# Recording the second half of a transformer block, with its buffers, for the builder that orders all engines

## The chip, the cores and the metric

The kernel runs on one core of one Trainium2 chip. A core has a matrix engine (TensorE, PE in the profile; its weight loads are PEld), a vector engine (VectorE, DVE), a scalar engine (ScalarE, ACT), a general engine (GpSimd, POOL) and SyncE (SP), which here only issues DMA transfers. Each engine works its own queue strictly in the order written by the program; engines wait for each other by semaphores. The metric is the device time of one execution in microseconds (us), lower is better; several executions are timed and their median is given.

## What is computed

One layer (DEPTH is 1) on x of 512 tokens by 1024. Cut to what matters here:

```python
h = h + jnp.concatenate([o_a, o_b, o_c], axis=-1) @ w_out[i]
h = h + conv_gated_mlp(rms_norm(h, ln_ffn[i]), w_up[i], conv_w[i], conv_b[i], w_down[i])
gate = jax.nn.sigmoid(rms_norm(h, ln_ple[i]) @ w_ple_gate[i])
h = h + (p[i] @ w_ple_proj[i]) * gate
```

Ahead of the first line stand a norm, one input projection and three kinds of attention (8 pairs of heads, A0 to C2). The MLP projects up to 2 x 2816 columns, puts a causal depthwise convolution of width 3 over the tokens, takes silu(gate) * val and projects down.

## The kernel before

**Precision by pairs.** Each matrix operand is split into a rounded high part and a low rest: `split` (line 408) has ACT write `hi` and DVE write `lo` = raw - `hi`. A product is then three matmuls, hi·hi, hi·lo, lo·hi (`mm3`, line 425). Weights land in raw tiles (`wraw`) from the SP queue, and PE reads `whi` and `wlo`. `Th` and `Tl` are the pairs of the activations, transposed.

**First half, up to line 1045.** While a `Plan` object is open, every call of an engine is recorded as an `Op` with the regions that it reads and writes. `Plan.due` gives PE's operations due times in program order (with a table of shifts per group, `SHIFT`), and works back from them for the others. `Plan.solve` then walks a model with prices per operation: of the operations that are ready at an engine it takes the one that is due first, and it lets DVE and POOL not use SBUF at once (`port`). `PLAN.pop().emit()` (line 1045) issues everything in that order. This Plan ends with the sixth of eight input blocks (k = 0 to 5) of the output projection.

**The end of the output projection, norm, projection of p (lines 1040 to 1184).** `last_out(t)` adds the input blocks k = 6 and 7 for token tile t (4 tiles of 128), both column halves n, in PSUM banks z and s. `ffn_norm(t)` computes the MLP's norm; `ffn_cols(t)` transposes it into `Th` and `Tl`; `ple_unit(n, t)` multiplies p with `w_ple_proj` and stores the result in DRAM (`pp_d`). Only PE is kept in program order here (`pe.pinned`); a scheduler of the framework places the work of ACT, DVE, POOL and SP, also in front of recorded work of the first half.

**MLP and gate (lines 1186 to 1886).** 22 column blocks f. Most are plain; f = 5, 10 and 15 are computed with seven instead of eight block products (`seven_weights`), whose sums of weights are made by adding DMAs and POOL. The down projection (`Down`, `down_weights`) uses the same scheme and names its blocks a1, t1, t2, b2, t3, a2, t4; its last part (phases 2 and 3) has weights in tiles `dn...`, sums of them by POOL, and adds each product onto `h` (`add_h`, on DVE, from a PSUM bank). `xh`/`xl` and `g..ah`/`g..al` are the pairs of the MLP's inner values. `cols3` transposes the finished `h`, and `gate` multiplies with `w_ple_gate`, takes the sigmoid and adds. Here a planner (`trial`, line 1856, and the loop behind it) orders tasks by hand-set costs, and the order in which it calls them is the order of all five queues (line 1869).

**Buffers.** Six raw tiles go round: four `wraw`, and two that reuse the room of one `whi` and one `wlo` (`in_turn`, line 394); seven of eight hi and lo tiles go round for splits. The pool `mp` (line 1049) opens in the room of the first half's pool; its tag `conv` has ten buffers, handed out in turn as new tiles.

Of the kernel before, what the change touches and what calls it, by code (L numbers as in the profile page):

```python
# [15 lines left out]
P = 128  # L16
D = 1024
S = 512
# [49 lines left out]
}  # L68


class Op:


# [5 lines left out]
class Plan:  # L79
# [2 lines left out]
    WRITES = ("out", "accum_out")  # L82
    LEAD = {"act": 0.035, "dve": 0.035, "pool": 0.095, "pe": 0.055, "sp": 0.1}

    def __init__(self, clock, there):
        self.group = "first"
        self.clock, self.there, self.ops, self.mem = clock, [(v.tensor.name, self.region(v), t) for v, t in there], [], {}

    @staticmethod
    def region(v):  # L90
        size = 2 if v.dtype == BF16 else 4
        (row, pn), *rest = [tuple(x) for x in v.ap]
        if v.tensor.space == bass.MemoryType.DRAM:
            return 0, 1, 0, 1
# [10 lines left out]
    def add(self, eng, name, a, k):  # L105
        op = Op(eng, name, a, k)
        named = [("out" if i == 0 and "out" not in k else "in", v) for i, v in enumerate(a)] + list(k.items())
        seen = [(key in self.WRITES, v) for key, v in named if hasattr(v, "tensor")]
        op.outs, op.ins = [v for w, v in seen if w], [v for w, v in seen if not w]
        op.ready = 0.0  # L110
        for w, v in sorted(seen, key=lambda x: x[0]):
            r = self.region(v)
            p0, p1, c0, c1 = r
            log = self.mem.setdefault(v.tensor.name, [])
            for other, (q0, q1, d0, d1), t in self.there:
                if other == v.tensor.name and c0 < d1 and d0 < c1:
                    op.ready = max(op.ready, t)
            keep = []
            for rec in log:
                other, w2, (q0, q1, d0, d1) = rec  # L120
                hit = p0 < q1 and q0 < p1 and c0 < d1 and d0 < c1
                if hit and (w or w2) and other is not op:
                    op.deps.append(other)
                if not (w and other is not op and p0 <= q0 and q1 <= p1 and c0 <= d0 and d1 <= c1):
                    keep.append(rec)
            keep.append((op, w, r))
            self.mem[v.tensor.name] = keep
        op.deps = list(dict.fromkeys(op.deps))
        op.pos, op.group = len(self.ops), self.group
        self.ops.append(op)  # L130
        self.price(op)

    def price(self, op):
        e, k = op.eng.name, op.k
        n = self.width(op.outs[0])
        cols = sum(1 for v in op.ins if self.width(v) == 1) - (op.name == "reciprocal")
        acc = "accum_out" in k
        op.move = 0
        if e == "pe":
            if op.name == "transpose":  # L140
                op.busy = 0.109
            else:
                op.busy = n * 0.0004556 + 0.001 if op.ins[0].dtype == F32R else n * 0.0017
            op.lag = 0.165
        elif e == "act":
            op.busy, op.lag = 0.06 + n * 0.00088 + (0.18 + 0.04 * cols if acc else 0.09 * cols), 0.1
        elif e == "dve":
            n = max([n] + [self.width(v) for v in op.ins])
            op.busy, op.lag = 0.07 + n * 0.001045 * (1 + (op.name == "tensor_tensor_scan")) + 0.06 * cols, 0.083
        elif op.name == "dma_start":  # L150
            op.move = n * 4 * op.outs[0].shape[0]
# [15 lines left out]
    ENGINES = ("dve", "pe", "act", "pool", "sp")  # L167

    def due(self, shift):
        t = 4.5  # L170
        for op in self.ops:
            if op.eng.name == "pe":
                op.dl = t + shift.get(op.group, 0.0)
                t += op.busy
        for op in reversed(self.ops):
            if op.eng.name != "pe":
                spent = op.busy + op.lag + 0.05 + (op.move / self.HW + 2.0 if op.move else 0.0)
                op.dl = min([q.dl for q in op.next], default=t) - spent

    def solve(self):  # L180
# [11 lines left out]
        while True:  # L192
# [44 lines left out]
        assert len(order) == len(self.ops)  # L237
        return order

    def emit(self):  # L240
        for op in self.ops:
            for d in op.deps:
                d.next.append(op)
        for op in self.choose():
            op.eng.now(op.name, op.a, op.k)

    def choose(self):
        self.due(SHIFT)
# [4 lines left out]
def kernel(ctx: ExitStack, tc: tile.TileContext, x, xt0, xt, pt_in, small, g_ffn_in, bias_c,  # L253
# [13 lines left out]
    ps = ctx.enter_context(tc.tile_pool(name="ps", bufs=1, space=bass.MemoryType.PSUM))  # L267

    PLAN = []

    class Engine:

# [20 lines left out]
    class Fixed:  # L293
# [5 lines left out]
        def tile(self, shape, dt, tag, bufs=1, name=None):  # L299
# [11 lines left out]
            kind, t = self.made[key]  # L311
            v = t[: shape[0], :n]
            if kind != dt:
                v = v.bitcast(dt)
            if len(shape) == 3:
                v = v.rearrange("p (a b) -> p a b", a=shape[1])
            return v

        def again(self, tag, bufs, dt):
# [74 lines left out]
    def in_turn(what, n):  # L394
        ring = RING[what]
        if len(ring) < n:
            tag = what
# [6 lines left out]
        return ring[-1]  # L404

    def raw_tile():
        return in_turn("raw", NRAW)
# [650 lines left out]
    nc.sync.dma_start(out=g_ffn, in_=g_ffn_in)  # L1058
    HN = {}

    def ffn_norm(t):

        token_stats(t, h[:, t, :], mtmp(BF16, 2, f"n2_sq{t}"))
        HN[t] = []
        for g in range(2):
            c = slice(g * S, (g + 1) * S)
            hn = mtmp(F32, 1, f"n2_hn{t}_{g}")
            dve.scalar_tensor_tensor(hn, h[:, t, c], rstd[:, t, 2:3], g_ffn[:, c], ALU.mult, ALU.mult)
            HN[t].append(hn)

    def ffn_cols(t):
        for g in range(2):
# [5 lines left out]
    def ple_cols():  # L1078

        pin = [mtmp(F32, 1, f"pin{k}") for k in range(2)]  # L1080
        for k in range(2):
            nc.sync.dma_start(out=pin[k], in_=pt_in[k])
# [7 lines left out]

    def ple_load(n, k):
        t = raw_tile()
        nc.sync.dma_start(out=t[:, :S], in_=w_ple_proj[k * P : (k + 1) * P, n * S : (n + 1) * S])
        WPP[n, k] = split(t, S)

    def ple_unit(n, t):
# [6 lines left out]
        nc.sync.dma_start(out=pp_d[t, n], in_=pp)  # L1103

    U = {}

# [6 lines left out]
    Xh, Xl = (mp.tile([P, 4, 4, H], F32R, tag=tag, name=tag) for tag in ("xh", "xl"))  # L1113
    for f in SEVEN:
        w = bass.AP(cols.tensor, cols[:, C_CONV0 + NF + f : C_CONV0 + NF + f + 1].offset, [cols.ap[0], [2 * NF, 3]])
        nc.gpsimd.tensor_scalar(w, w, -1.0, 1.0, ALU.mult, ALU.mult)
    XA = {}

    def keep_cols(t, g, pt):
# [467 lines left out]
    old("pin")  # L1587
    old("left")
    xa = old("left")
    old("conv")  # L1590
    HNS = {(2, 0): old("conv"), (2, 1): old("conv")}
    old("conv", 3)
    HNS.update({(3, 0): old("conv"), (3, 1): old("conv")})
    old("conv", 2)
    for tag in ("z", "s", "t", "o"):
        old(tag, COUNT[tag])
    old("raw", 4)
# [352 lines left out]
```

## Time and profile before

| | us |
|---|---|
| median of 3 runs (lowest, highest) | 721.74 (720.13, 722.8) |
| the profiled execution | 721.91 |
| its span, first to last instruction | 720.0 |
| PE busy in the span | 702.6 |
| DVE busy | 557.5 |
| ACT busy | 389.8 |
| POOL busy | 268.3 |
| mean granted TensorE clock | 0.997 |

All engines run at once, so busy times don't add up. In a row of the timeline stand the start, the duration, the engine, the line and the operation with output and inputs; in brackets the idle time of the engine just before, and what ended it. Line 286 is the one line through which all recorded and wrapped calls go, so the names of tiles tell operations apart. Matmuls overlap: a 512-column one lasts about 0.39 us, while the next one starts 0.23 us after it.

### The profile page before, as it was taken

To read this page: it belongs to the slowest core of one execution; us is meant where nothing else is said; L and a number is where in the kernel's file an instruction comes from. 1 tells how busy PE (TensorE), PEld (TensorE's weight loads), DVE (VectorE), ACT (ScalarE), POOL (GpSimd) and SP (SyncE) were. 2 spreads that over 40 slices of the span, in tenths; PEclk is the share of its full clock that TensorE was granted. 3 is DMA by queue.
4 is the path that set the end of the run, shared out by engine and by line. 5 is a ranking of instruction groups with operands and counts; after the bars stand their busy time and mean duration, and the time that the engine had idled before them with its cause. 6 is when DMAs were issued, how large, how long until landed. Compare 5 with 4: busy or idle time off the path is not lost. (4 is left out here: it accounts for less than half of the span.)

```text
span 720.0 us, 11793 instructions
## 1 busy us (share of the span) xinstructions
PE 702.6 (98%) x4204; PEld 633.6 (88%) x4204; DVE 557.5 (77%) x1090; ACT 389.8 (54%) x745; POOL 268.3 (37%) x355
## 2 busy tenths in 40 slices
PE   7999999999999999899999999999999999989997
PEld 7999999999999887698888899888998888889886
DVE  7788898888887755758789778797988789986552
ACT  6657685575676644745555444454445443434821
POOL 3687676847666621203003331113410023280400
PEclk9999999999999999999999999999999999999999
DMA  9533552314112245454536325541362323113441
GB/s 323 201 99 89 142 136 91 103 53 130 68 55 66 67 124 160 140 175 111 162 104 145 103 89 178 130 117 45 103 203 77 117 66 118 42 55 102 154 124 59
DMA packets 36951, 83.22 MB, mean 116 GB/s; under 512 B 4215, under 2 KB 6263, under 8 KB 36893
## 3 DMA queue, kind: packets, MB, share of 16 engines
q1 hardware_dynamic: 32844, 73.52, 32.1%
q0 software_dynamic: 3760, 8.66, 6.5%
q8 instruction: 33, 0.54, 0.3%
q10 hardware_dynamic: 288, 0.30, 0.1%
q14 instruction: 26, 0.21, 0.1%
HBM read 74.19 MB, written 4.21 MB: 109 GB/s over the span
## 5 line engine op out<-in xcount | busy, mean ns | idle before, releaser
L286 PE MATMUL z<-whi,Th 128*128 128x384 f32 (+2 forms) x356 | 123.6, 356 | 6.0 <-ACT whi L286 4.5
L286 ACT CAST whi<-wraw 128x768 fp32r<-128x768 f32 (+2 forms) x132 | 98.5, 766 | 52.4 <-POOL wraw L286 23.2
L286 PE MATMUL z<-wlo,Th 128*128 128x384 f32 (+2 forms) x356 | 122.0, 352 | 0.0
L286 PE MATMUL z<-whi,Tl 128*128 128x384 f32 (+2 forms) x356 | 121.7, 351 | 0.0
L286 DVE TENSOR_TENSOR wlo<-wraw,whi 128x768 fp32r<-128x768 f32 (+2 forms) x114 | 105.0, 936 | 16.6 <-ACT whi L286 16.2
L286 PEld LDWEIGHTS z<-whi,Th 128*128 128x128 f32 x356 | 67.5, 190 | 10.7 <-ACT whi L286 4.5
L286 PEld LDWEIGHTS z<-whi,Tl 128*128 128x128 f32 x356 | 67.1, 189 | 4.6 <-DVE Tl L286 0.4
L286 PEld LDWEIGHTS z<-wlo,Th 128*128 128x128 f32 x356 | 67.3, 190 | 3.3
L286 PE MATMUL z<-Th,whi 128*128 128x512 f32 (+1 forms) x180 | 66.3, 368 | 1.4 <-ACT pps L286 1.4
L286 PE MATMUL s<-Th,whi 128*128 128x512 f32 (+1 forms) x180 | 66.2, 368 | 0.0
L286 PE MATMUL z<-Tl,whi 128*128 128x512 f32 (+1 forms) x180 | 66.1, 367 | 0.0
L286 PE MATMUL s<-Tl,whi 128*128 128x512 f32 (+1 forms) x180 | 66.0, 367 | 0.0
L286 PE MATMUL z<-Th,wlo 128*128 128x512 f32 (+1 forms) x180 | 66.0, 367 | 0.0
L286 POOL TENSOR_TENSOR wraw<-wraw,wraw 128x768 f32<-128x768 f32 (+1 forms) x14 | 26.1, 1877 | 107.0 <-DVE wlo L286 93.6
L286 PE MATMUL s<-Th,wlo 128*128 128x512 f32 (+1 forms) x180 | 66.0, 366 | 0.0
L286 ACT ACTIVATE e<-e,st 128x128 f32<-128x128 f32 (+3 forms) x80 | 44.6, 559 | 15.9 <-DVE st L286 15.5
L286 POOL TENSOR_TENSOR rs<-rs,nhalf 128x4 f32<-128x4 f32 x40 | 43.2, 1090 | 4.9 <-DVE rs L286 1.4
L286 PE MATMUL t<-wlo,g_ah 128*128 128x256 f32 x150 | 42.4, 282 | 0.3 <-DVE wlo L286 0.3
L286 PE MATMUL t<-whi,g_ah 128*128 128x256 f32 x150 | 42.3, 282 | 0.3 <-DVE h L286 0.3
L286 DVE SCALAR_TENSOR_TENSOR c<-z,cols,c 128x511 f32<-128x511 f32 (+1 forms) x38 | 28.4, 748 | 18.0 <-ACT c L286 17.4
L286 PE MATMUL t<-whi,g_al 128*128 128x256 f32 x150 | 42.3, 282 | 0.0
L286 PEld LDWEIGHTS z<-Th,whi 128*128 128x128 f32 x180 | 33.8, 188 | 7.9 <-ACT pps L286 1.8
(337 smaller groups left out, 1955.9 us busy)
## 6 DMA issues: line engine op xcount, KB each, us to landing
wraw<-in_w_up_dram SPq DMA_DIRECT2D x33, 384.0 KB, 3.8
wraw<-in_w_in_dram SPq DMA_DIRECT2D x28, 384.0 KB, 3.8
wraw<-in_w_down_dram SPq DMA_DIRECT2D x17, 384.0 KB, 3.0
whi_again<-in_w_up_dram SPq DMA_DIRECT2D x12, 384.0 KB, 3.7
wraw<-in_w_out_dram SPq DMA_DIRECT2D x16, 256.0 KB, 2.9
wraw<-in_w_up_dram SPq DMA_DIRECT2D x13, 256.0 KB, 3.1
wlo<-wraw POOLq DMA_DIRECT2D x7, 384.0 KB, 5.0
wraw<-in_w_ple_gate_dram SPq DMA_DIRECT2D x10, 256.0 KB, 2.9
```

Of the source, the lines that this page charges most:

```text
L286: ins = getattr(self.eng, op)(*a, **k)
```

## The change

The second half is recorded too. After the first Plan has been issued, a second one opens; it takes over the first one's clocks and its log of regions, and it ends behind the loop of the MLP's planner, whose tasks now only record. So the planner's order becomes the program order that `due` reads, and `solve` sets the order of all five engines from the end of the output projection to the last store. `SHIFT` has no entry for it. The line that issues has become line 319.

- `mp` is now of the kind `Fixed`: each buffer of a tag is one tile for good, and reuse is ordered by regions. Since a tile has one type, a placeholder in DRAM (`StandIn`) is recorded where a float32 buffer is later used as float32r, and is replaced by a real tile when issued.
- The two extra raw tiles now take the room of the first `whi` and `wlo` tiles (number 0), which the end of the output projection doesn't read; the round of splits then uses numbers 1 to 7.
- The last of four loads of `w_ple_proj` moves behind `last_out(3)`, and `ffn_cols(1)` ahead of the projections of p for n = 1.
- The norm's scratch goes into the buffer of its first result instead of one of its own.
- The model charges 1.3 us for the first silu or sigmoid.

```diff
+class StandIn:
+    def __init__(self, place, make):
+        self.place, self.make, self.tile = place, make, None
...
-    def __init__(self, clock, there):
-        self.group = "first"
-        self.clock, self.there, self.ops, self.mem = clock, [(v.tensor.name, self.region(v), t) for v, t in there], [], {}
+    def __init__(self, clock, there=(), mem=None, fresh=0.0):
+        self.group, self.loaded, self.fresh = "first", set(), fresh
+        self.clock, self.there, self.ops, self.mem = clock, [(v.tensor.name, self.region(v), t) for v, t in there], [], mem or {}
...
                 if hit and (w or w2) and other is not op:
-                    op.deps.append(other)
+                    if other.end is None:
+                        op.deps.append(other)
+                    elif not eng.name == other.eng.name == "pe":
+                        op.ready = max(op.ready, other.end)
...
+            f = k.get("func", op.a[2] if len(op.a) > 2 else None)
+            if f in (AF.Silu, AF.Sigmoid) and f not in self.loaded:
+                self.loaded.add(f)
+                op.busy += 1.3
...
             if what == "raw" and len(ring) >= W["raw"]:
-                tag = ("hi", "lo")[(len(ring) - W["raw"]) % 2]
-            t = pi.tile([P, 768], F32 if tag == "raw" else F32R, tag=f"w{tag}", bufs=W[tag])
-            ring.append(t if tag == what else pi.again(f"w{tag}", W[tag], F32))
+                ring.append(MORE_RAW.pop(0))
+            else:
+                ring.append(pi.tile([P, 768], F32 if what == "raw" else F32R, tag=f"w{what}", bufs=W[what]))
...
-    PLAN.pop().emit()
+    first = PLAN.pop()
+    first.emit()
     p1.__exit__(None, None, None)
...
-    mp = ctx.enter_context(tc.tile_pool(name="mp", bufs=1, side="right", reuse_waits="tile"))
+    mp = Fixed(ctx.enter_context(tc.tile_pool(name="mp", bufs=1, side="right", reuse_waits="tile")))
+    for q in ("hi", "lo"):
+        pi.tile([P, 768], F32R, tag=f"w{q}", bufs=W[q])
+        MORE_RAW.append(pi.again(f"w{q}", W[q], F32))
+    PLAN.append(Plan(first.last, (), first.mem, first.last["dve"] + 0.6))
...
-    for n in range(2):
-        for k in range(2):
-            ple_load(n, k)
+    for n, k in ((0, 0), (0, 1), (1, 0)):
+        ple_load(n, k)
     last_out(0)
...
     last_out(3)
+    ple_load(1, 1)
     ffn_norm(3)
+    ffn_cols(1)
     for t in range(2):
         ple_unit(1, t)
-    ffn_cols(1)
+    mp.turn["conv"] += 2
...
-    act.pinned = dve.pinned = pool.pinned = sp.pinned = True
     order = [q for q in TASKS if q.end is None]
...
         order.remove(q)
+    PLAN.pop().emit()
```

Three places show what moves. The first is PE at the start of `last_out`. In the names, whi_4/wlo_4 are the weights of block k = 6 for n = 0, whi_5/wlo_5 of k = 6 for n = 1, and whi_6 and whi_7 those of k = 7; z_0, s_1, z_1, s_0 are banks. Before:

```order
L286 MATMUL z_0_128<-whi_4_117,Th1_65 128x512
L286 MATMUL z_0_128<-wlo_4_118,Th1_65 128x512
L286 MATMUL z_0_128<-whi_4_117,Tl1_67 128x512
L286 MATMUL z_0_128<-whi_6_123,Th1_65 128x512
L286 MATMUL z_0_128<-wlo_6_124,Th1_65 128x512
L286 MATMUL z_0_128<-whi_6_123,Tl1_67 128x512
L286 MATMUL s_1_131<-whi_5_120,Th1_65 128x512
```

The same place on PE after:

```order
L319 MATMUL z_0_128<-whi_4_117,Tl1_67 128x512
L319 MATMUL s_1_131<-whi_5_120,Th1_65 128x512
L319 MATMUL s_1_131<-wlo_5_121,Th1_65 128x512
L319 MATMUL s_1_131<-whi_5_120,Tl1_67 128x512
L319 MATMUL z_1_129<-whi_4_117,Th1_65 128x512
L319 MATMUL z_1_129<-wlo_4_118,Th1_65 128x512
L319 MATMUL z_1_129<-whi_4_117,Tl1_67 128x512
L319 MATMUL s_0_130<-whi_5_120,Th1_65 128x512
L319 MATMUL s_0_130<-wlo_5_121,Th1_65 128x512
L319 MATMUL z_0_128<-whi_6_123,Th1_65 128x512
```

Before, three matmuls of k = 6 stand ahead of the first of k = 7; now eleven do, from four banks.

The second place is the SP queue behind the last load for the output projection (pt_in is p, transposed; w_up0 and w_up1 are the MLP's first two column blocks). Before:

```order
L1093 DMA wraw_3_125<-in_w_ple_proj_dram 128x512
L286 DMA wraw_0_116<-in_w_up0_dram 128x512
L286 DMA wraw_1_119<-in_w_up1_dram 128x768
L286 DMA wraw_2_122<-in_w_up1_dram 128x768
L286 DMA wraw_3_125<-in_w_up1_dram 128x512
L1058 DMA g_ffn_3053<-in_g_ffn_in_dram 128x1024
L1082 DMA pin0_3060<-in_pt_in_dram 128x512
L1082 DMA pin1_3061<-in_pt_in_dram 128x512
```

The SP queue after:

```order
L319 DMA wraw_3_125<-in_w_ple_proj_dram 128x512
L319 DMA conv_0_3058<-in_pt_in_dram 128x512
L319 DMA conv_1_3059<-in_pt_in_dram 128x512
L319 DMA pin_0_3055<-in_g_ffn_in_dram 128x1024
L319 DMA whi_0_again_3052<-in_w_up0_dram 128x768
L319 DMA wlo_0_again_3053<-in_w_up0_dram 128x768
```

The two loads of p stood behind four loads of up weights; now they lead, and the first up block follows into the two extra raw tiles.

The third place is DVE where the last down products of column half n = 0 end and `cols3` begins (the rows `h<-h,t` are `add_h`, the rows `wlo<-` are splits of weights). Before:

```order
L286 TENSOR_TENSOR h<-h,t_149 128x2x256
L286 TENSOR_TENSOR h<-h,t_150 128x2x256
L286 TENSOR_TENSOR wlo_113<-dn_1_a_5958,whi_112 128x512
L286 TENSOR_TENSOR wlo_115<-wlo_again,whi_114 128x768
L286 TENSOR_TENSOR wlo_118<-dn_1_a_5923,whi_120 128x512
L286 TENSOR_TENSOR h<-h,t_149 128x2x256
```

DVE after:

```order
L319 TENSOR_TENSOR wlo_115<-conv_3069,whi_114 128x512
L319 TENSOR_TENSOR h<-h,t_149 128x2x256
L319 TENSOR_TENSOR h<-h,t_150 128x2x256
L319 TENSOR_TENSOR wlo_118<-wlo_again,whi_117 128x768
L319 TENSOR_TENSOR wlo_121<-conv_3065,whi_120 128x512
L319 TENSOR_TENSOR h<-h,t_149 128x2x256
```

One of the three splits has moved in front of the two sums. On PE, the two sets of four transposes of `cols3` that stood side by side there have six matmuls of the next product between them now.

More of the change, by code (lines that the diff above doesn't have):

```diff
@@ L68, with real @@
 }
+STAND_INS = {}
+class StandIn:
+    def __init__(self, place, make):
+        self.place, self.make, self.tile = place, make, None
+def real(v):
+    s = STAND_INS.get(v.tensor.name) if isinstance(v, bass.AP) else None
+    if s is None:
+        return v
+    if s.tile is None:
+        s.tile = s.make()
+    t = s.tile[:, :]
+    r = bass.AP(t.tensor, v.offset, v.ap)
+    return r if r.dtype == v.dtype else r.bitcast(v.dtype)
 class Op:
@@ L92, in region @@
         (row, pn), *rest = [tuple(x) for x in v.ap]
-        if v.tensor.space == bass.MemoryType.DRAM:
-            return 0, 1, 0, 1
+        if v.tensor.space == bass.MemoryType.DRAM and v.tensor.name not in STAND_INS:
+            return 0, 1, v.offset * size, (v.offset + (pn - 1) * row + sum((n - 1) * st for st, n in rest) + 1) * size
         p0, c0 = divmod(v.offset, row)
@@ L113, in add @@
             p0, p1, c0, c1 = r
-            log = self.mem.setdefault(v.tensor.name, [])
+            where = STAND_INS[v.tensor.name].place if v.tensor.name in STAND_INS else v.tensor.name
+            if where not in self.mem and v.tensor.space != bass.MemoryType.DRAM:
+                op.ready = max(op.ready, self.fresh)
+            log = self.mem.setdefault(where, [])
             for other, (q0, q1, d0, d1), t in self.there:
@@ L126, in add @@
             keep.append((op, w, r))
-            self.mem[v.tensor.name] = keep
+            self.mem[where] = keep
         op.deps = list(dict.fromkeys(op.deps))
@@ L169, in due @@
     def due(self, shift):
-        t = 4.5
+        t = max(4.5, self.clock["pe"])
         for op in self.ops:
@@ L237, in solve @@
         assert len(order) == len(self.ops)
+        self.last = clock
         return order
@@ L244, in emit @@
         for op in self.choose():
-            op.eng.now(op.name, op.a, op.k)
+            op.eng.now(op.name, [real(v) for v in op.a], {q: real(v) for q, v in op.k.items()})
     def choose(self):
@@ L269 @@
     PLAN = []
+    STAND_INS.clear()
     class Engine:
@@ L311, in tile @@
             kind, t = self.made[key]
+            if kind == F32 and dt == F32R:
+                key = tag, i % bufs, "r"
+                if key not in self.made:
+                    size = [P, t.shape[1]]
+                    tag = f"{tag}_{i % bufs}"
+                    d = dp.tile(size, F32R, tag=f"{tag}_r", name=f"{tag}_r")
+                    STAND_INS[d[:, :].tensor.name] = StandIn(t[:, :].tensor.name, lambda: self.pool.tile(size, F32R, tag=tag, name=f"{tag}_real"))
+                    self.made[key] = F32R, d
+                kind, t = self.made[key]
             v = t[: shape[0], :n]
@@ L404, in in_turn @@
         return ring[-1]
+    MORE_RAW = []
     def raw_tile():
@@ L1081, in ple_cols @@
         for k in range(2):
-            nc.sync.dma_start(out=pin[k], in_=pt_in[k])
+            sp.dma_start(out=pin[k], in_=pt_in[k])
         hl = [mp.tile([P, 7, H], F32R, tag=tag, bufs=3, name=f"pT_{tag}").rearrange("p j c -> p (j c)") for tag in ("ah", "al")]
@@ L1092, in ple_load @@
         t = raw_tile()
-        nc.sync.dma_start(out=t[:, :S], in_=w_ple_proj[k * P : (k + 1) * P, n * S : (n + 1) * S])
+        sp.dma_start(out=t[:, :S], in_=w_ple_proj[k * P : (k + 1) * P, n * S : (n + 1) * S])
         WPP[n, k] = split(t, S)
@@ L1589 @@
     xa = old("left")
[L1590 to L1594, printed above, removed]
+    HNS = {}
+    for t in (3, 2):
+        old("conv", 2)
+        HNS.update({(t, g): old("conv") for g in range(2)})
+        old("conv", 0 if t == 3 else 2)
     for tag in ("z", "s", "t", "o"):
```

17 lines of the change are left out of this document (8 added, 9 removed).

## The prediction, made before the changed kernel ran

> **What bounds the kernel now.** I read the page's table of engines first, then stretches of the span, then PE's timeline at every stretch in which PE is not full, and there the rows of the engine that it waits for.
>
> ```profile
> PE 702.6 (98%) x4204; PEld 633.6 (88%) x4204; DVE 557.5 (77%) x1090; ACT 389.8 (54%) x745; POOL 268.3 (37%) x355
> ```
>
> PE is the bound: an order can only win what PE loses to waits. The columns of the next view are the stretch, its length, then busy us of PE, PEld, DVE, ACT and POOL, the granted clock, and DMA.
>
> ```profile
> 20.00:260.00 240.00, 239.66 (x1490) 225.90 (x1489) 198.87 (x588) 161.98 (x394) 163.18 (x247) 1.00 0.36 100
> 260.00:320.00 60.00, 56.06 (x318) 47.28 (x317) 35.79 (x55) 28.84 (x50) 7.27 (x14) 1.00 0.49 157
> 320.00:600.00 280.00, 279.67 (x1613) 244.20 (x1613) 229.37 (x317) 137.32 (x203) 56.14 (x39) 1.00 0.40 112
> 600.00:665.00 65.00, 60.88 (x451) 57.96 (x450) 55.01 (x65) 27.70 (x42) 24.12 (x13) 0.97 0.25 82
> 665.00:720.00 55.00, 50.87 (x266) 42.76 (x264) 23.96 (x37) 20.81 (x34) 8.97 (x21) 1.00 0.37 117
> ```
>
> The recorded first half (20 to 260) loses 0.34 us, the MLP (320 to 600) 0.33. What can be won lies in two places, both in what is newly recorded: 3.94 us between 260 and 320, the end of the output projection and the norm, and 4.12 us between 600 and 665, where the down projection's last part passes into the gate. The last stretch's 4.13 us are the end after the last matmul, which no order shortens.
>
> **The change part by part.** Instructions are the same in number and kind; only their places differ. I measure each wait from start to start, less the usual step, since a modelled end hides some of it.
>
> *A, the last values.* The first matmul of block k = 7 waits for ACT and DVE to split the output of the last pair.
>
> ```profile
> 276.42 0.39 PE L286 MATMUL z<-whi,Th 128*128 128x512 f32 x1
> 276.65 0.40 PE L286 MATMUL z<-wlo,Th 128*128 128x512 f32 x1
> 276.89 0.39 PE L286 MATMUL z<-whi,Tl 128*128 128x512 f32 x1
> 278.71 0.50 PE L286 MATMUL z<-whi,Th 128*128 128x512 f32 x1 [1.43 <-ACT Th L286]
> 278.04 0.62 ACT L286 CAST Th<-oall 128x512 fp32r<-128x512 f32 x1 [0.83 <-DVE oall L286]
> 278.69 0.69 DVE L286 TENSOR_TENSOR Tl<-oall,Th 128x512 fp32r<-128x512 f32 x1 [0.68 <-ACT Th L286]
> ```
>
> The wait costs 278.71 - 276.89 - 0.23 = 1.59. Afterwards 11 matmuls of k = 6 stand ahead instead of 3; 8 x 0.23 = 1.84 covers it. Th is there at 278.66, and the first k = 7 matmul comes at 276.42 + 11 x 0.23 = 278.95; the first use of Tl is the 15th matmul, at 279.64, and Tl ends at 279.38. The three splits of `w_ple_proj` that ACT and DVE did in front of this chain now come behind it; they are needed 36 matmuls after 276.42, at 284.7, so they have 5 us. Won: 1.59.
>
> *B, p.* The second pair of p comes late.
>
> ```profile
> 273.90 3.73 SPq L286 DMA_DIRECT2D wraw<-in_w_up_dram  x4
> 279.83 0.90 SPq L1082 DMA_DIRECT2D pin<-in_pt_in_dram  x2
> 285.24 1.22 ACT L286 CAST pT_ah<-pin 128x512 fp32r<-128x512 f32 x2 [2.00 <-DMA pin<-in_pt_in_dram]
> 285.95 0.69 DVE L286 TENSOR_TENSOR pT_al<-pin,pT_ah 128x512 fp32r<-128x512 f32 x1 [2.49 <-ACT pT_ah L286]
> 288.48 0.68 DVE L286 TENSOR_TENSOR pT_al<-pin,pT_ah 128x512 fp32r<-128x512 f32 x1
> 287.70 0.39 PE L286 MATMUL z<-wlo,pT_ah 128*128 128x512 f32 x1
> 289.22 0.50 PE L286 MATMUL z<-whi,pT_al 128*128 128x512 f32 x1 [1.12 <-DVE pT_al L286]
> wraw<-in_w_ple_gate_dram SPq DMA_DIRECT2D x10, 256.0 KB, 2.9
> ```
>
> Price: 289.22 - 287.70 - 0.23 = 1.29. The loads of p were issued at 279.83 behind four loads of up weights and landed after 5.4 us; they now lead, and a load of that size usually lands in 2.9. They can't be issued before room opens as Tl ends (279.38), so they land near 282.4 and 282.9. On DVE the two splits are neighbours now, where 285.95 and 288.48 lay 2.5 apart. With ACT busy with one norm square first, both are split near 285.5, and PE, which comes 1.59 earlier, asks for the first near 285.4. Won: 1.29, with about 0.2 at risk.
>
> *C, a bank.* `first` waits until ACT has emptied bank z.
>
> ```profile
> 303.62 0.39 PE L286 MATMUL s<-whi,pT_al 128*128 128x512 f32 x1
> 305.39 0.39 PE L286 MATMUL z<-Th,whi 128*128 128x256 f32 x1 [1.38 <-ACT pps L286]
> 304.74 0.60 ACT L286 COPY pps<-z 128x512 f32<-128x512 f32 x1
> ```
>
> Price: 305.39 - 303.62 - 0.23 = 1.54. Before, 12 matmuls and two sets of transposes lie between the bank's last write and its next use; afterwards 18 matmuls, 4.1 us. ACT places this copy ahead of the norm square of tile 3, and the casts of the first up weights come sooner, as those are loaded sooner. I take 1.3, for ACT is dense here and the moved fourth load of `w_ple_proj` leaves PE little room at its use. A to C: 4.42 at stake, 4.0 taken.
>
> *D, the order in the MLP.* For 280 us PE stays close to the old program order, but 256-column matmuls of two banks now alternate. That costs nothing by the rows where the first half does it already (step 0.12):
>
> ```profile
> 64.76 0.28 PE L286 MATMUL z<-wlo,Th 128*128 128x256 f32 x1
> 64.88 0.28 PE L286 MATMUL s<-k,q 128*128 128x256 f32 x1
> ```
>
> A bank that alternates ends up to 12 x 0.12 = 1.4 us later, and ACT's and DVE's chain behind it with it. Here nothing can be won beyond 0.33. The loss lies between 0 and the worst that any order made in such a stretch, 4.12; the nearest row is the recorded first half's 0.34 in 240, but that had a table of shifts, and this has none. I take 0.8, so 0.5 net.
>
> *E and F, the passage to the gate.* First a split of down weights is late, then a sum into h, whose bank the transposes of `cols3` need.
>
> ```profile
> 620.64 0.38 PE L286 MATMUL o<-whi,xh 128*128 128x256 f32 x1
> 622.21 0.38 PE L286 MATMUL o<-wlo,xh 128*128 128x256 f32 x1 [1.19 <-DVE wlo L286]
> 620.62 1.54 DVE L286 TENSOR_TENSOR wlo<-dn_a,whi 128x512 fp32r<-128x512 f32 x1
> 639.84 0.60 PE L286 MATMUL t<-ident,h 128*128 128x128 f32 x4
> 643.08 0.66 PE L286 MATMUL t<-ident,h 128*128 128x128 f32 x4 [2.64 <-DVE h L286]
> 643.49 0.37 PE L286 MATMUL z<-whi,xh 128*128 128x256 f32 x1
> 637.08 1.17 DVE L286 TENSOR_TENSOR wlo<-dn_a,whi 128x512 fp32r<-128x512 f32 x1
> 640.13 2.29 DVE L286 TENSOR_TENSOR wlo<-dn_a,whi 128x512 fp32r<-128x512 f32 x1
> 642.35 0.68 DVE L286 TENSOR_TENSOR h<-h,t 128x512 f32<-128x512 f32 x1
> 639.36 2.52 POOL L286 TENSOR_TENSOR wraw<-wraw,wraw 128x768 f32<-128x768 f32 x1
> 644.00:646.00 2.00, 2.00 (x13) 2.00 (x13) 2.00 (x1) 0.37 (x1) 2.00 (x2) 0.62 0.00 0
> 646.00:648.00 2.00, 2.00 (x12) 2.00 (x11) 2.00 (x4) 0.46 (x1) 1.30 (x1) 0.53 0.00 0
> ```
>
> E costs 622.21 - 620.64 - 0.12 = 1.45. F costs 643.08 - 639.84 - 0.41 (a set of transposes, 643.49 - 643.08) = 2.83, and then the clock is granted at 0.62 and 0.53 for 4 us: 2 x 0.38 + 2 x 0.47 = 1.70. Together 5.98. DVE's splits are slow because POOL sums at the same time (2.29 beside a POOL sum, where the sum from PSUM takes 0.68). Afterwards the `dn` splits of E stand ahead of the pairs xl, so E goes. At F one split of 637.08 (1.1 us) has moved ahead and six matmuls (0.7) lie between: 2.83 - 1.1 - 0.7 = 1.0 is left; but PE comes 1.45 sooner by E, while POOL's sums need not, so up to 2.5. I take 1.7, without the slow clock, since pauses of 1.29 to 1.59 (A to C) left the clock at 1.00 in their stretch. Won: 5.98 - 1.7 = 4.3.
>
> [...]
>
> *The end.* The last two half tiles of the gate alternate; the first ends nearer to the second, at most 0.1.
>
> Sum: 4.0 + 4.3 - 0.5 - 0.1 = 7.7. The profiled execution took 721.91, of which 720.0 are span; it stands 0.17 above the median of 721.74. The prediction is made for the median: 714.0.
>
> **The rivals.**
>
> *1, the passage keeps its waits.* POOL's sums for the last down products are as many as before, and DVE's splits of two SBUF tiles still fall beside them. If DVE's sum into h stays as late, E and F remain: 721.74 - 4.0 + 0.6 = 718.3; if only E goes, 716.9. For it speaks 55.01 of 65 us of busy DVE; against it, that the split and the matmuls did move. [...]
>
> *2, slower: sums of weights come late.* At f = 5 and 15 POOL now has its first own sum in front of the second or third adding DMA, and POOL waits there until the first DMA has landed; the second and third start up to 5.0 us later.
>
> ```profile
> wlo<-wraw POOLq DMA_DIRECT2D x7, 384.0 KB, 5.0
> 337.10 1.45 POOL L286 TENSOR_TENSOR wlo_again<-wlo_again 128x256 f32<-128x256 f32 x1
> 353.81 0.28 PE L286 MATMUL s<-xh,whi 128*128 128x256 f32 x1
> ```
>
> Before, the last sum for f = 5 ends at 338.55 and its weights are used at 353.81: 15.3 us, of which a cast and a split take under 2. So 5.0 is hidden, and the change turns slower only if other lateness of 8 us joins it. Each such pause would cost what F does, 4.5; two of them leave 714.0 + 9.0 = 723.0, three 727.5.
>
> *3, nothing moves.* The waits are replaced one for one, the gain of A to C being eaten in the MLP, where DVE is at 229.37 of 280: D at its bound of 4.12, rival 1 besides, 721.74 - 4.0 + 4.1 = 721.8.
>
> **How the numbers follow.** The forecast, 711 to 716.5, has 0.62; rival 1 (716.5 to 719) 0.18; rival 2 (723 to 728) 0.13; rival 3 (719 to 723) 0.07. Half a per cent, about what a measurement of this kernel can tell, is 3.6 us: 718.1 to 725.3. Faster: 0.62 and two thirds of rival 1, 0.74. Slower: most of rival 2, 0.11. Same: 0.15. If all waits went, 4.42 + 5.98 + 0.33 = 10.7 would leave 711.0; the range takes 710.7 as its low end and reaches through rival 1 to 719.5, which holds 0.8.
>
> **What would show it.** A: no wait for ACT Th near 277. B: p's loads issued as the first DMAs after 279.4, landed within 3.5 us. C: `first` begins near 301 instead of 305.4. D: PE full to within 1 us over the 280 us. E and F: the two sets of transposes with six matmuls between them, a pause there under 2 us, no granted clock under 1.00. Wrong: a pause over 2.6 us with a slow clock behind it anywhere in the MLP or at the passage, or PE waiting for casts between 300 and 320 because SP's mixed stores of pps and loads of weights stand in each other's way.

## The result, and the profile after

The changed kernel takes 717.69 us (median of 6 runs, 717.28 to 718.5) where the kernel before takes 721.64 (6 runs, 720.13 to 722.8): a ratio of 0.9947, 95% interval 0.9932 to 0.9962. It is faster, by 3.95 us, about half of the 7.7 us that were forecast, and 3.7 us slower than the predicted 714.0. The time lies outside the forecast's 711 to 716.5 and inside 710.7 to 719.5 only because that reached through rival 1. The profiled execution has a span of 716.1 us, 3.9 less than before.

PE is busy for 701.1 us of it (702.6 before). Three stretches of the changed kernel, to be read beside those that the prediction showed of the kernel before (columns as there):

```profile
260.00:320.00 60.00, 60.00 (x362) 52.63 (x361) 39.46 (x61) 31.35 (x54) 9.40 (x18) 1.00 0.49 160
320.00:600.00 280.00, 278.68 (x1587) 242.15 (x1586) 227.41 (x318) 140.04 (x204) 56.90 (x39) 1.00 0.41 117
600.00:665.00 65.00, 60.71 (x464) 59.15 (x463) 50.54 (x62) 30.10 (x47) 23.40 (x21) 0.95 0.28 89
```

Between 260 and 320 PE is full: the 3.94 idle us of the kernel before are gone. Between 320 and 600 it now loses 1.32 instead of 0.33. Between 600 and 665 it loses 4.29 instead of 4.12, and the clock is lower, 0.95 instead of 0.97: where 4.3 us were to be won, nothing was. What PE waits for most in the whole execution (waited for, then us in total, times, longest):

```profile
PE z L319 <- ACT whi L319: 4.6, 1, 4.6
PE t L319 <- DVE h L319: 4.3, 1, 4.3
PE z L319 <- DVE conv L319: 1.2, 2, 0.6
```

The first row is the start of the kernel. The second is one single pause. Its place in the timeline of the changed kernel, PE first (some rows left out), then DVE, then POOL, then the two stretches of 5 us with the clock (a row with x2 holds two instructions):

```profile
629.49 0.40 PE L319 MATMUL t<-whi,xl 128*128 128x256 f32 x2
634.18 0.76 PE L319 MATMUL t<-whi,ah 128*128 128x256 f32 x2 [4.29 <-DVE h L319]
640.30 0.60 PE L319 MATMUL t<-ident,h 128*128 128x128 f32 x4
625.81 7.02 DVE L319 TENSOR_TENSOR wlo<-wraw,whi 128x768 fp32r<-128x768 f32 x1 [0.18 <-ACT whi L319]
632.76 0.68 DVE L319 TENSOR_TENSOR wlo<-conv,whi 128x512 fp32r<-128x512 f32 x1
633.36 1.27 DVE L319 TENSOR_TENSOR h<-h,t 128x512 f32<-128x512 f32 x2
624.07 0.61 POOL L319 DMA_DIRECT2D conv<-pp_d  x1 [1.72 <-DVE wlo L319]
624.69 1.31 POOL L319 TENSOR_TENSOR conv<-conv,conv 128x512 f32<-128x512 f32 x1
625.93 1.85 POOL L319 TENSOR_TENSOR wraw<-wraw,wlo_again 128x768 f32<-128x768 f32 x1
627.73 1.29 POOL L319 TENSOR_TENSOR conv<-conv,conv 128x512 f32<-128x512 f32 x1
628.97 1.83 POOL L319 TENSOR_TENSOR wraw<-wraw,wraw 128x768 f32<-128x768 f32 x1
630.76 1.26 POOL L319 TENSOR_TENSOR conv<-conv,conv 128x512 f32<-128x512 f32 x1
630.00:635.00 5.00, 0.82 (x4) 0.85 (x5) 5.00 (x5) 0.60 (x1) 4.04 (x3) 0.79 0.00 0
635.00:640.00 5.00, 5.00 (x26) 5.00 (x26) 2.63 (x2) 0.83 (x1) 2.08 (x2) 0.52 0.18 56
```

A DVE split of 128x768 that takes 0.95 us elsewhere takes 7.02 here: it ends 0.81 us after the last of a row of five POOL sums, of which four began after it did. Of the splits that the small programs below set beside such a row none takes more than 2.59; this one let four sums pass. Behind it on DVE stand a second split and the two sums into h, and the product at 634.18 adds onto the bank that the first of these sums reads. PE loses 634.18 - 629.49 - 0.24 = 4.45 us (the expectations below say 4.57, from the step of one matmul instead of two). After that the 15 rows of two matmuls up to the transposes take 640.30 - 634.18 = 6.12 instead of 15 x 0.24 = 3.6, at a clock of 0.52: another 2.5. The pause costs 7.0.

The waits of 0.6 in the third row have the same form: a split of 2.50 us beside a POOL sum stands on DVE ahead of the convolution step that empties the bank.

```profile
407.16 1.85 POOL L319 TENSOR_TENSOR whi_again<-wlo_again,whi_again 128x768 f32<-128x768 f32 x1
407.33 2.50 DVE L319 TENSOR_TENSOR wlo<-wraw,whi 128x768 fp32r<-128x768 f32 x1 [4.01 <-ACT whi L319]
409.75 1.52 DVE L319 SCALAR_TENSOR_TENSOR conv<-z,cols,conv 128x511 f32<-128x511 f32 x2
411.42 0.47 PE L319 MATMUL z<-Th,whi 128*128 128x512 f32 x1 [0.61 <-DVE conv L319]
```

### The profile page after: what moved, and what is told of

It is laid out like the page before. It is cut to its first block, busy times and chain, and to the rows that moved or that the text cites. A ratio compares the mean times of both kernels' runs of the same rounds, so it can differ in the third digit from the quotient of the medians.

```text
span 716.1 us, 11807 instructions
## 1 busy us (share of the span) xinstructions
PE 701.1 (98%) x4204; PEld 633.7 (88%) x4204; DVE 551.7 (77%) x1090; ACT 392.4 (55%) x745; POOL 265.9 (37%) x355
## 4 chain that ended last, share of the span: by engine, by line
PE 95%; DVE 2%; issue 1%; ACT 1%; POOL 1%; DMA 0%; POOLq 0%
PE z L319 49%; PE s L319 23%; PE t L319 15%; PE o L319 7%; DVE wlo L319 1%; DVE conv L319 1%; DMA zn<-in_w_in_dram 0%; ACT whi L319 0%; POOL e L319 0%; ACT conv L319 0%; POOL rs L319 0%; POOL wlo L319 0%; DVE oall L319 0%; DVE h L319 0%; ACT otmp L319 0%
## 5 line engine op out<-in xcount | busy, mean ns | idle before, releaser
L319 DVE TENSOR_TENSOR wlo<-wraw,whi 128x768 fp32r<-128x768 f32 (+2 forms) x114 | 110.6, 980 | 24.0 <-ACT whi L319 23.7
L319 DVE TENSOR_TENSOR conv<-conv,conv 128x512 f32<-128x512 f32 (+1 forms) x31 | 21.7, 705 | 23.9 <-ACT conv L319 23.8
L319 PEld LDWEIGHTS s<-Th,wlo 128*128 128x128 f32 x180 | 33.8, 188 | 6.2
L319 PEld LDWEIGHTS s<-Tl,whi 128*128 128x128 f32 x180 | 33.8, 188 | 6.1
L319 PEld LDWEIGHTS z<-Th,wlo 128*128 128x128 f32 x180 | 33.8, 188 | 6.1
```

Of the source, the lines that this page charges most:

```text
L319: ins = getattr(self.eng, op)(*a, **k)
```

## The experiments

**The order on DVE, at one place, at two, at four.** If the pause comes only from what stands ahead of the sums into h on DVE, it can be removed by moving two instructions. A function behind the builder's `solve` takes instructions of one engine from the order and puts them back behind a later one; all other queues keep their order.

```diff
+    LATER = (("dve", 397, 398, 400),)
+    def hold(self, order):
+        for eng, first, last, behind in self.LATER:
+            mine = [op for op in order if op.eng.name == eng]
+            goal = mine[behind]
+            for x in mine[first : last + 1]:
...
     def emit(self):
...
-        for op in self.choose():
+        order = self.choose()
+        if self.fresh:
+            order = self.hold(order)
+        for op in order:
```

Numbers count DVE's instructions of the second Plan: 397 and 398 are the two splits, 399 and 400 the two sums.

> In the changed kernel's profile DVE's split wlo<-wraw,whi at 625.81 takes 7.02 us beside four sums of POOL, the two sums into h stand behind it on DVE, and PE waits until 634.18. Here the two sums into h go in front of that split and of the next one (wlo<-conv,whi); nothing else moves on any engine. Theory P (POOL's back-to-back sums hold up a DVE split of two SBUF tiles, not a sum that reads PSUM, and h is late only because it is queued behind such a split): the loss of 4.57 us and the slow clock behind it (13 pairs of matmuls at 0.43 instead of 0.238, 2.5 us) go, 717.7 - 7.1 = 710.6. What may be late next: at the transposes of cols3 the sum into h still stands behind two other splits, which now meet POOL's sums; if that costs what it cost in the kernel before (2.83 and 1.7 of slow clock), 715.1. Rival B (the bank t is late because two products alternate in it and end late, whatever stands ahead on DVE): the pause stays over 3 us, 717.7.

Measured: 716.8 us (714.3 to 718.35), a ratio of 0.9946 (0.9922 to 0.997). The pause at 630 is gone, and the place that the expectation named as the next one costs nearly as much. Its timeline, DVE and then PE:

```profile
630.85 2.35 DVE L341 TENSOR_TENSOR wlo<-wraw,whi 128x768 fp32r<-128x768 f32 x1
633.12 0.68 DVE L341 TENSOR_TENSOR wlo<-conv,whi 128x512 fp32r<-128x512 f32 x1
633.72 2.58 DVE L341 TENSOR_TENSOR wlo<-wlo_again,whi 128x768 fp32r<-128x768 f32 x1
636.22 1.75 DVE L341 TENSOR_TENSOR wlo<-conv,whi 128x512 fp32r<-128x512 f32 x1
637.89 0.67 DVE L341 TENSOR_TENSOR h<-h,t 128x512 f32<-128x512 f32 x1
634.51 0.40 PE L341 MATMUL z<-whi,xl 128*128 128x256 f32 x2
638.62 0.72 PE L341 MATMUL t<-ident,h 128*128 128x128 f32 x4 [3.71 <-DVE h L341]
```

This is the kernel before's pause at the transposes again: two splits beside POOL's sums ahead of the sum into h, a loss of 638.62 - 634.51 - 0.24 = 3.87. In the changed kernel PE came to it 7 us late, and so it did not show. As ratios to the kernel before, this run and the changed kernel are the same, 0.9946 and 0.9947.

The second run also moves that sum ahead of its two splits (`("dve", 401, 402, 403)` is added).

> As the run before, and the sum into h for the transposes of cols3 also goes in front of the two splits ahead of it (wlo<-wlo_again,whi and wlo<-conv,whi). Theory P: no pause over 1 us between 600 and 665 and no granted clock under 1.00 there, 710.6. Rival B: 717.7, or 716.9 if only the second pause is of the order.

Measured: 711.27 us (710.94 to 711.53), a ratio of 0.9865 (0.9833 to 0.9897). PE waits for no sum into h any more. The third run adds the two places in the MLP (`("dve", 156, 156, 158)` and `("dve", 248, 248, 250)`).

> As the run before, and at the two places in the MLP where PE loses 0.77 us each to a bank (411 and 497), DVE's split of 2.50 us beside a POOL sum goes behind the two convolution steps that empty the bank. Theory P: another 2 x 0.77 = 1.5 us, 709.1. Rival B: as the run before, since the bank's chain would be late for its own length.

Measured: 709.62 us (709.22 to 709.76), a ratio of 0.9842 (0.981 to 0.9874), 1.65 less than with two places, where 1.5 was expected. The two stretches of this kernel:

```profile
320.00:600.00 280.00, 279.90 (x1596) 243.53 (x1595) 225.83 (x321) 141.27 (x205) 56.79 (x39) 1.00 0.42 118
600.00:665.00 65.00, 65.00 (x504) 62.65 (x503) 50.72 (x71) 36.87 (x57) 26.28 (x29) 1.00 0.35 111
```

PE is full, the clock is 1.00. Six instructions in other places on one queue are worth twice what the whole change brought. Rival B of these runs, that the banks' own chains are late, falls.

**POOL's sums left out.** The other side of the same cause: the order on DVE stays, and four sums go.

```diff
-        for op in self.choose():
+        order = self.choose()
+        if self.fresh:
+            sums = [op for op in order if op.eng.name == "pool" and op.k.get("op") == ALU.subtract]
+            order = [op for op in order if op not in sums[-6:-2]]
+        for op in order:
```

> The changed kernel without four of POOL's sums of down weights, those that run from 625.93 to 632.02; the products of the last column half that use them are computed with unsummed weights. The order on all other engines stays. Theory P: the split at 625.81 takes under 1.3 us at the same place of DVE's queue, the pause falls under 1 us, 710.6. Rival B: the split gets short, the pause stays over 3 us, 717.7. A third possibility, that the load of pp_d issued on POOL's queue at 624.07 holds DVE up: the split stays near 7 us, 717.7.

Measured: 711.82 us (711.21 to 712.1), a ratio of 0.987 (0.9832 to 0.9909). The same split at the same place:

```profile
626.65 1.01 DVE L323 TENSOR_TENSOR wlo<-wraw,whi 128x768 fp32r<-128x768 f32 x1 [0.18 <-ACT whi L323]
```

1.01 instead of 7.02, and PE waits for no sum into h any more. The load of pp_d is still on POOL's queue, with one sum behind it, so the load alone does not hold the split: it takes the four sums. Whether it also takes the load, together with a row of sums, this run does not tell; the end of this section comes back to it.

**A rule of the builder instead of numbers.** The model lets a POOL sum wait until DVE has left SBUF. At 625.93 in the trace above it was POOL that went first: its sum took 1.85 us, the split 7.02. One condition lets only DVE wait:

```diff
-        when = lambda q: max(q.at, held[other[q.eng.name]]) if q.port else q.at
+        when = lambda q: max(q.at, held[other[q.eng.name]]) if q.port and (q.eng.name == "dve" or not self.fresh) else q.at
```

> The changed kernel with one rule of the builder's model changed for the second half: a sum of POOL no longer waits until DVE has left SBUF, DVE's split still waits for POOL. The order that comes out moves splits on DVE (E's and F's among them), sums on POOL and some matmuls; one split of 128x768 still stands ahead of the two sums into h. Theory P: the pause at 630 stays as long as that split meets POOL's row of sums, 717; if the split now falls between two rows of sums, as the model has it, the pause goes and the time is 709 to 712. Rival B as before, 717.7.

Measured: 711.24 us (711.05 to 711.6), a ratio of 0.9862 (0.9847 to 0.9877). The passage:

```profile
600.00:665.00 65.00, 65.00 (x504) 62.64 (x503) 54.71 (x71) 36.10 (x56) 27.90 (x28) 1.00 0.35 112
```

It is free of pauses here; the two waits in the MLP stay. A split still stands ahead of the two sums into h; it begins at 626.52 and takes 2.05, so it got a turn. This order also issues the load of pp_d behind that row of sums, at 636.24, which matters at the end of this section. The gain is one order's; one run does not show that the rule is better in general.

**The changed kernel and the best order on one chip.**

> The changed kernel itself, for a comparison on one chip: 0.9947 of the time before, the pause of over 4 us at 630 with its 7 us split.

> The run with all four places reordered again, beside the changed kernel on one chip: 8 us below it (4.57 and 2.5 of slow clock at 630, 1.5 at the two places in the MLP), 0.983 of the time before.

Measured: 717.64 us (717.22 to 718.34), a ratio of 0.9962 (0.9943 to 0.9981), and 709.84 us (709.63 to 710.04), a ratio of 0.9848 (0.983 to 0.9866): 7.8 us between the two. In the profile of the repeated changed kernel the split again takes 7 us, so this is no accident of one execution:

```profile
625.54 7.03 DVE L319 TENSOR_TENSOR wlo<-wraw,whi 128x768 fp32r<-128x768 f32 x1 [0.18 <-ACT whi L319]
```

**The passage alone.** Two runs were meant to leave A to C to the builder and to give the MLP and the gate the order of the kernel before, by a chain through each engine's instructions from a point on.

```diff
+        last = {}
+        for op in self.ops[self.fixed :] if self.fresh else ():
+            if op.eng.name in last and last[op.eng.name] not in op.deps:
+                op.deps.append(last[op.eng.name])
+            last[op.eng.name] = op
```

In the first, `fixed` is the MLP's first instruction:

> The changed kernel, but from the first column block of the MLP to the end each engine keeps the order in which the tasks are recorded, which is the order that the kernel before has there on all five queues; only the end of the output projection, the norm and the projection of p are left to the builder. If the gain of the change lies in this passage alone (steps A to C, 4.4 us lost before, all of it won), and E and F come back as before: no wait between 260 and 320, about 4.2 us less than before, 0.994 of it, as the changed kernel. If the MLP's and the gate's new order brings a net gain of its own: more than 1 us slower than the changed kernel. If it costs: faster than the changed kernel by what D lost, 1 to 1.5 us.

Measured: 724.08 us (722.48 to 725.64), a ratio of 1.0043 (1.0031 to 1.0055). In the second, it is the first matmul behind the first two column blocks:

> As the run that fixed the order from the MLP's first block on, but the fixing begins behind the first two column blocks; ahead of it the MLP's first loads, casts and splits are ordered by the builder among the work of the passage. From there to the end the order is that of the kernel before. If what spoiled the passage in that run was the place of the MLP's first loads on the SP queue (p's loads issued at 279.58 instead of 273.25): no wait over 0.5 us between 260 and 320, E and F as before, 717.0 where before has 721.2 (0.994). If p's second load, which here stands behind one load of up weights, is late again: 718.5. If the passage needs the whole new order: 721 or more.

Measured: 728.24 us (728.04 to 728.85), a ratio of 1.0105 (1.0082 to 1.0127). The passage has new waits in both, so what the first run was to show fell away, and of the second one's cases only the last came, 721 or more. In the first run p's loads come behind a load of up weights, which waits for room, and its split is late again; in the second run PE waits for a copy by ACT. The SP queue and PE of the first run, then PE of the second:

```profile
273.43 0.43 SPq L324 DMA_DIRECT2D whi_again<-in_w_up_dram  x1
279.58 0.91 SPq L324 DMA_DIRECT2D conv<-in_pt_in_dram  x2
293.21 0.50 PE L324 MATMUL z<-whi,al 128*128 128x512 f32 x1 [2.15 <-DVE al L324]
```

```profile
306.98 0.39 PE L324 MATMUL s<-Th,whi 128*128 128x256 f32 x1 [4.24 <-ACT conv L324]
```

So these runs do not price A to C by themselves: where the two orders meet, more is lost than the passage had lost before (4.36 and 5.95 idle us between 260 and 320, where it was 3.94). What they do show is that E and F belong to the order of the MLP and the gate. With that order put back, both return, with the same values in both runs (rows of the first):

```profile
PE t L324 <- DVE h L324: 3.0, 2, 2.6
PE o L324 <- DVE wlo L324: 1.2, 1, 1.2
```

**DVE's split beside POOL's sums, by itself.** SBUF is the memory that holds the tiles, PSUM the one that holds the banks. Three small programs start a split of 128x768 at different moments of a row of POOL sums. A sum that reads PSUM runs ahead of the split on DVE and sets its start. The core of it:

```diff
+    for n in sums:
+        keep(nc.gpsimd.tensor_tensor(out=c[:, :n], in0=a[:, :n], in1=b[:, :n], op=ALU.subtract))
+    keep(nc.vector.tensor_tensor(out=d[:, :w], in0=y[:, :w], in1=bank[:, :w], op=ALU.add))
+    keep(nc.vector.tensor_tensor(out=lo, in0=s, in1=hi.bitcast(F32), op=ALU.subtract))
```

> No part of the layer is computed, the output is zeros. A DVE split of 128x768 (two SBUF inputs) is started at different times after POOL has begun one, two or five sums (128x512 and 128x768 in turn, as in the changed kernel); ahead of it a sum that reads PSUM sets its start. Theory P in its strong form (POOL keeps the way to SBUF as long as its queue has sums): the split ends about 0.8 us after POOL's last sum, 8 us for a start early in a row of five. In its weak form (the split waits for the sum that runs and then gets its turn): never more than 1.9 + 0.95 = 2.8 us. Rival (no sharing): 0.95 us always.

> No part of the layer is computed, the output is zeros. The split of the first port measurement again, but begun in steps of 0.02 us between 0.8 and 1.3 us after POOL's first sum (128x512, 1.3 us) of five, so that it meets the last third of that sum; in the changed kernel the 7.02 us split began 1.12 us after a sum of 1.31 us. If a split that begins in a sum's last 0.3 us loses its turn for the whole row: 7 us for starts from about 1.0 to 1.28. If it loses one turn only: 0.2 + 1.85 + 0.8 = 2.8 us there. If it always gets the next turn: 0.95 to 1.3 us.

> No part of the layer is computed, the output is zeros. The port measurement once more, with own input and output tiles for each of POOL's five sums, as the changed kernel has them (in the two measurements before, all sums wrote one tile, which may have kept them apart by a moment). If sums of different tiles follow each other so closely that a split which begins near a switch loses its turn for the rest of the row, as in the changed kernel: 3 to 7 us for some of the starts. If not: at most 2.6 us for all starts, and what made the split of the changed kernel lose four turns in a row stays open.

Of 96 splits in trials with sums none takes more than 2.59 us. The splits of the three programs (one of each program is without sums), with the least, the median and the longest in ns:

```profile
L107 DVE TENSOR_TENSOR lo<-raw,hi x34: 949/2002/2542, 9.9 to 208.6; 128x768 fp32r<-128x768 f32 x34
```

```profile
L107 DVE TENSOR_TENSOR lo<-raw,hi x27: 949/1017/1576, 9.9 to 228.2; 128x768 fp32r<-128x768 f32 x27
```

```profile
L109 DVE TENSOR_TENSOR lo<-raw,hi x38: 949/1193/2590, 19.6 to 319.1; 128x768 fp32r<-128x768 f32 x38
```

Two trials of the third program, POOL and DVE in turn:

```profile
171.00 5.59 POOL L102 TENSOR_TENSOR m<-m,m 128x768 f32<-128x768 f32 x3
171.00 0.95 DVE L109 TENSOR_TENSOR lo<-raw,hi 128x768 fp32r<-128x768 f32 x1
179.35 3.73 POOL L102 TENSOR_TENSOR m<-m,m 128x768 f32<-128x768 f32 x2
179.38 2.59 DVE L109 TENSOR_TENSOR lo<-raw,hi 128x768 fp32r<-128x768 f32 x1
```

The split that begins together with a sum of 128x768 (171.00) takes 0.95 us, as the one without sums does; the one that begins 0.03 us behind such a sum (179.38) takes 2.59, a little less than that sum (1.80 in the first program) and a split of 0.95 one after the other. The measured times are those of theory P's weak form (at most 2.8 us), not of its strong one (8 us). Why the split of the changed kernel loses four turns in a row stays open. It is not the moment of its start alone, nor whether the sums share a tile, for both were varied here.

The small programs leave one thing out that goes with it in the traces: a DMA that POOL itself issues right in front of the row of sums, in the changed kernel the load of pp_d at 624.07. The kernel before has such a place too, which neither the prediction nor the experiments used. DVE, then POOL:

```profile
388.94 4.38 DVE L286 TENSOR_TENSOR g_al<-sm,g_ah 128x1024 fp32r<-128x1024 f32 x1
388.53 0.87 POOL L286 DMA_DIRECT2D wlo_again<-in_w_up_dram  x1 [6.45 <-DVE c L286]
389.09 1.06 POOL L286 TENSOR_TENSOR wraw<-wraw 128x256 f32<-128x256 f32 x1
391.18 1.04 POOL L286 TENSOR_TENSOR whi_again<-whi_again 128x256 f32<-128x256 f32 x1
```

A split of this size takes 1.22 us elsewhere (407.94, same kernel); here it lets four sums of POOL pass. In the traces of the kernel before and of the changed kernel, 388.94 and 625.81 are the only places where a DVE instruction lets a sum of tiles pass that began after it. Both rows of sums stand right behind such a DMA, and the splits end 1.10 and 0.81 us after the row's last sum. The split at 630.85 above (2.35 us) lets one sum pass, the last of the row behind the load of pp_d. Where the load stands behind the row, in the order of the rule with POOL first, the split took 2.05, and in the small programs, which have no such DMA, 2.59 at most. No run keeps the row of sums and takes the DMA away, so that the DMA is a condition is not shown.

## Why the prediction was right and wrong

**A, B, C: right, and a little better than taken.** No wait for Th, p or the bank is left. 4.42 were at stake, 4.0 taken, all won. `first` begins at 300.20, where "near 301" was forecast. In B the way was another one: p's loads did not have to wait for room.

```profile
273.25 0.91 SPq L319 DMA_DIRECT2D conv<-in_pt_in_dram  x2
283.91 1.29 DVE L319 TENSOR_TENSOR al<-conv,ah 128x512 fp32r<-128x512 f32 x2
285.19 0.39 PE L319 MATMUL z<-whi,al 128*128 128x512 f32 x1
```

They were issued at 273.25, not behind 279.38, since the fixed buffers put p into room that was already free. The splits end at 285.20 (forecast near 285.5), and PE asks for the first at 285.19 (forecast 285.4).

**D: right in size, not in its reason.** Net 0.5 was forecast to be lost. One matmul of the output projection and one convolution step late in the MLP, first of the kernel before, then of the changed one:

```profile
256.67 0.63 PE L286 MATMUL z<-whi,Th 128*128 128x512 f32 x2
587.74 1.53 DVE L286 SCALAR_TENSOR_TENSOR c<-z,cols,c 128x511 f32<-128x511 f32 x2 [1.54 <-ACT c L286]
```

```profile
256.33 0.63 PE L319 MATMUL z<-whi,Th 128*128 128x512 f32 x2
583.45 0.75 DVE L319 SCALAR_TENSOR_TENSOR conv<-z,cols,conv 128x511 f32<-128x511 f32 x1 [2.50 <-ACT conv L319]
```

The changed kernel is 0.34 ahead at the first (this varies between executions: the run with two places, which has the changed kernel's order up to there and beyond, issues the load of pp_d at 624.68, 0.61 behind the changed kernel's 624.07) and 4.29 at the second. With 4.42 won by A to C, D cost 0.34 + 4.42 - 4.29 = 0.5. Its two visible waits were not those of the forecast's reason, alternating banks, but splits beside POOL sums. These two alone cost 1.65 by the run that moves them, so the rest of the stretch was about 1.1 quicker, where 0.33 was forecast: that the sum of 0.5 came out is luck. "PE full to within 1 us" was missed by 0.3.

**E: right.** The 1.45 are gone, and with them a wait of 0.29 behind it that the prediction had left out.

**F: this is the step that failed.** The prediction took the pause at the transposes, subtracted the split that had moved and the six matmuls between, and left 1.7 without a slow clock. At the transposes that is even too much: PE passes them at 640.30 without a wait. But 10 us earlier, at the product that adds onto bank t, stands a new pause with a slow clock, 7.0 us. E and F were to give 4.3; before, the passage lost 5.98 and 0.45 with that small wait, so 7.0 - 6.4 = 0.6 was lost instead: the term put at 1.7 measured 7.0. Summed up, 0.34 at the start, 4.42 by A to C, 0.5 lost in D and 0.6 here give 3.7; the span is 3.9 shorter.

Half of the reason was in the prediction's rows: a split of two SBUF tiles beside a POOL sum took 2.29 where it takes 0.69 alone. It was used as a fixed surcharge on the splits that had it before. The order says which split stands ahead of which sum on DVE, but not against which POOL sum it will run. POOL's row of sums came to lie beside another split, one with 17 us to spare (its weights are used at 642.95), with an urgent sum into h queued behind it. That a split can let a whole row of sums pass was not in those rows, but in the trace of the kernel before, at 388.94. That the sums hold up the splits is rival 1's mechanism, and the measured 717.69 lies between its two values, 716.9 and 718.3; as the pause stands at another place and is longer, the closeness of the number is partly luck. E went, as in its second value; F was still there, hidden behind the new pause, as the run with one place reordered shows.

**The sign named for a wrong forecast**, a pause over 2.6 us with a slow clock behind it at the passage, is what came: a pause of 4.45, and a clock of 0.50 from 632.93 to 639.76. The runs with a fixed order add two shorter waits. In the second, a wait of 2.11 us ends at 351.66; the 256-column matmuls behind it begin 0.12 us apart at first, 0.21 apart from 352.23 to 355.43 (as at the clock of 0.50 in the kernel before, 644.53 to 645.17) and 0.12 apart again, and the stretch from 340 to 400 has a mean clock of 0.97. In the first, the wait of 2.15 that ends at 293.21 left the clock at 1.00 (260 to 320). So the length of a wait alone does not decide whether the clock falls; what else does is open.

**Rivals 2 and 3** did not come: PE waits nowhere for the weights of f = 5 and 15, and the gain of A to C was not eaten in the MLP.

## What to carry to other kernels

An instruction of DVE with two SBUF inputs had no fixed price beside POOL's sums (0.95 to 7.03 us for one size): ask of each one that stands ahead of an urgent instruction what POOL does at that time, and let work that has time stand behind the urgent one. When a pause is removed, look at the next place of the same form before counting the gain; here one moved pair gave almost nothing and two gave 6 us. The instructions of one queue that are worth moving are found in the trace behind the longest wait, not in the order.

## What was not expected of the hardware

- One split let four POOL sums pass (7.02 and 7.03 us in two profiles), while none of the 96 splits in the small programs took more than 2.59. The same happened to a split of 1.22 us in the kernel before (4.38). In the traces of the kernel before and of the changed kernel the row of sums stood right behind a DMA that POOL issued.
- The clock fell to 0.50 behind a pause of 2.83 us that ended at 643.08 (for 3.4 us, 644.49 to 647.90, in the kernel before) and in a pause of 4.45 us that ended at 634.18 (for 6.8 us, 632.93 to 639.76, in the changed kernel). Pauses of 1.29 to 1.59 left it at 1.00, a wait of 2.15 did in one run, and behind one of 2.11 in another the step of the 256-column matmuls went from 0.12 to 0.21 us for 3.2 us.
